# A decoder layer on one core: the first weights on another queue, gamma scaled on another engine, and the FFN input stage in token halves with its activations moved by 64 bytes

## The chip, the core and the metric

The kernel runs on one core of a Trainium2 chip. The metric is the device time of one execution in microseconds (us). The time before is the median of three runs, 662.29 us (661.71 to 663.59).

The core has a tensor engine (PE, its weight loads shown apart as PEld), a vector engine (DVE), a scalar engine (ACT), a general engine (POOL) and a synchronising engine (SP). DMAs are issued by SP, ACT or POOL, each from a queue of its own, in program order.

## The reference

One layer with 512 tokens of 1024 channels, all in float32:

```python
proj = h @ w_in                                  # q | k | v | pool_in | gate logits
mixed = sigmoid(g0) * (moba_attention(q, k, v, rel_bias) @ w_branch_attn) \
      + sigmoid(g1) * (multiscale_pool(p, w_pool_group, pool_scale) @ w_branch_pool)
h = layer_norm(ALPHA * h + mixed @ w_out, ln1_g, ln1_b)
a, u = split(h @ w_ffn_in, 2)                    # 1024 -> 2 x 2816
a = causal_dwconv(a, conv_w, conv_b)             # width 3
f = (gelu(a) * u) @ w_ffn_out                    # 2816 -> 1024
h = layer_norm(ALPHA * h + f, ln2_g, ln2_b)
```

Here `layer_norm` subtracts the mean, multiplies with one over the root of the variance plus epsilon, then with gamma, and adds beta.

## The kernel before

**Matmuls.** Each float32 product is made of three matmuls in float32r, which is a float32 rounded to fewer bits: every operand is split into a rounded part `hi` and a remainder `lo` (`split`, lines 63 to 68: ACT or another engine copies `hi`, DVE subtracts for `lo`), and `mm3` (lines 144 to 148) adds hi x hi, hi x lo and lo x hi in one bank of PSUM. The first argument of a matmul's name in the profile is the moving operand, of 512 or 256 columns, the second the 128x128 stationary one, which every matmul loads anew.

**Weights.** All weights come in chunks of 128 x 1024 in a fixed order (`chunks`, lines 78 to 88). `fetch` (lines 92 to 112) issues a chunk's DMA on SP's queue into one of three raw buffers and splits it into one of five pairs `whi`, `wlo`; `weights` keeps three chunks ahead. The first chunk alone is fetched in two parts of 512 columns, with the second half of the first activations loaded between them.

**Stages, in order.** (1) Start: eight matmuls on zeros warm the array (lines 167 to 169, `WARM`), while the activations `xT` and the first weights land; the v projection (line 240) comes first. (2) The remaining input projections run between the steps of the attention. (3) The branch projections, gated and added into `mx`. (4) The output projection per block of 128 tokens, followed by layer norm 1 (`ln1_vec`) and its transposition into `hT_hi` and `hT_lo` (`ln1_T`), which lie in the pool `hTp` (lines 456 to 459). (5) The FFN input, 44 tiles of 128 output channels: the weights are stationary, `hT` moves. The first five tiles are run over tokens 0 to 255, with the last two transposes between them, then over tokens 256 to 511; tiles 5 to 43 over all 512 tokens at once (lines 609 to 626). After each pair of tiles `gated` makes the convolution, gelu and product. (6) The FFN output as seven products of a Winograd scheme (`PRODUCTS`), whose weights are partly summed by DMA in `tw` (`fetch_fo`, lines 120 to 137; POOL issues those accumulating DMAs). (7) Layer norm 2 per block of 128 tokens: `scale_out`, `share_out` and, for the last block, `finish`.

**Layer norm.** `ln_rows` (lines 447 to 451) loads gamma and beta on POOL's queue to all partitions and multiplies gamma with -0.5 on ACT; it is called ahead of layer norm 1 and in the middle of stage 6, where SP also stores beta to the first 256 rows of the output for `scale_out` to add to. `moments` (lines 470 to 475) aggregates mean and variance on DVE, takes the root of variance plus epsilon on ACT, and adds epsilon to the variance in place on DVE; `invert` refines the inverse root from both.

**What sets the order.** Each engine runs its instructions in an order that the tile framework's scheduler fixes ahead; within `finish` the order is pinned. Semaphores do the rest.

Of the kernel before, what the change touches and what calls it, by code (L numbers as in the profile page):

```python
# [8 lines left out]
F32 = mybir.dt.float32  # L9
F32R = mybir.dt.float32r  # L10
AF = mybir.ActivationFunctionType
ALU = mybir.AluOpType
PSUM = bass.MemoryType.PSUM

P = 128
S = 512
D = 1024
KT = D // P
# [9 lines left out]
EPS = 1e-5  # L28
# [3 lines left out]
LEAD = 3  # L32
RING = 5
TMP = 4
WARM = 8
NKEEP = 12
NLATE = 4
KH = NF // 2
# [5 lines left out]
def layer_kernel(ctx: ExitStack, tc: tile.TileContext, xT, x, w_v, w_c, rel_bias, invcnt, w_group,  # L44
                 pscale, w_br, w_out, lnr, w_fi, convp, w_fo, out):
    nc = tc.nc
# [9 lines left out]
    def bank(name):  # L56
        return ps.tile([P, S], F32, tag="ps", name=name)
# [5 lines left out]
    def split(hi, lo, src, copy=None):  # L63
        if copy:
            copy(hi, src)
        else:
            nc.scalar.activation(hi, src, AF.Copy)  # L67
        nc.vector.tensor_tensor(lo, src, hi.bitcast(F32), op=ALU.subtract)  # L68
# [9 lines left out]
    chunks = [w_v[c] for c in range(4)]  # L78
# [13 lines left out]
    def fetch(pool=None, early=None):  # L92
        i = state["next"]
        state["next"] = i + 1
        if isinstance(chunks[i], tuple):
            ready[i] = fetch_fo(i, *chunks[i])
            return
        raw = wp.tile([P, D], F32, tag="wraw", name=f"wraw{i}", bufs=3)
        if pool is None:
            hi = wp.tile([P, D], F32R, tag="whi", name=f"whi{i}", bufs=RING)  # L100
            lo = wp.tile([P, D], F32R, tag="wlo", name=f"wlo{i}", bufs=RING)
        else:
            hi = pool.tile([P, D], F32R, name=f"whi{i}")
            lo = pool.tile([P, D], F32R, name=f"wlo{i}")
        parts = 2 if early else 1
        for c in range(parts):
            sl = slice(c * (D // parts), (c + 1) * (D // parts))
            nc.sync.dma_start(raw[:, sl], chunks[i][:, sl])
            split(hi[:, sl], lo[:, sl], raw[:, sl])
            if c == 0 and early:  # L110
                early()
        ready[i] = (hi, lo)

    def half(name, sl):
        return w_fo[int(name[1]) - 1, 2 - int(name[2])][:, sl]

    def piece(c):
        return slice(c * D, min((c + 1) * D, KH * S))

    def fetch_fo(i, name, c):  # L120
        sl = piece(c)
        n = sl.stop - sl.start
        step = {"T3": "=B11", "B11": "+B12", "T1": "+B22", "T2": "+B21", "T4": None}
        if name in step:
            raw = tw[:, sl]
        else:
            raw = wp.tile([P, D], F32, tag="wraw", name=f"wraw{i}", bufs=3)[:, :n]
            nc.sync.dma_start(raw, half(name, sl))
        hi = wp.tile([P, D], F32R, tag="whi", name=f"whi{i}", bufs=RING)[:, :n]
        lo = wp.tile([P, D], F32R, tag="wlo", name=f"wlo{i}", bufs=RING)[:, :n]  # L130
        split(hi, lo, raw)
        then = step.get(name)
        if then and then[0] == "+":
            nc.gpsimd.dma_start(raw, half(then[1:], sl), accum_op=ALU.add)  # L134
        elif then:
            nc.sync.dma_start(raw, half(then[1:], sl))
        return hi, lo

    def weights(i):
        while state["next"] <= min(i + LEAD, state["limit"]):  # L140
            fetch()
        return ready[i]

    def mm3(out_, w, a, start, stop, **kw):
        (wh, wl), (ah, al) = w, a
        nc.tensor.matmul(out_, wh, ah, start=start, stop=False, **kw)  # L146
        nc.tensor.matmul(out_, wh, al, start=False, stop=False, **kw)  # L147
        nc.tensor.matmul(out_, wl, ah, start=False, stop=stop, **kw)  # L148

    def split3(v, a):  # L150
        return tuple(t.rearrange("p (a c) -> p a c", a=a) for t in v)

    xT_hi = act.tile([P, KT, S], F32R, tag="actT_hi", name="xT_hi")
    xT_lo = act.tile([P, KT, S], F32R, tag="actT_lo", name="xT_lo")
# [12 lines left out]
    wb_ = bank("warm_ps")  # L167
    for i in range(WARM):
        nc.tensor.matmul(wb_, warm[:, :P], warm, start=True, stop=True)
# [58 lines left out]
    for kt in range(KT):  # L228
        wh, wl = split3(weights(kt // 2), 2)
        wh, wl = wh[:, kt % 2, :], wl[:, kt % 2, :]  # L230
# [189 lines left out]
    for f in range(KT):  # L420
        if f == KT - LEAD:
            state["limit"] = WO0 + RING - 1
        wh, wl = split3(weights(BR0 + f), KT)
# [4 lines left out]
        for br in (1, 0):  # L428
            b = bank(f"br{f}_{br}")
            for k in range(4):  # L430
                src = (zT_hi[:, k, :], zT_lo[:, k, :]) if br else (oT_hi[:, k, :], oT_lo[:, k, :])
                mm3(b, (wh[:, 4 * br + k, :], wl[:, 4 * br + k, :]), src, k == 0, k == 3)
            t = bp.tile([P, S], F32, tag="m", name=f"m{f}_{br}", bufs=4)
# [13 lines left out]
    def ln_rows(r):  # L447
        t = hw.tile([P, 2, D], F32, tag="lnb", name=f"lnb{r}")
        nc.gpsimd.dma_start(t, bass.AP(tensor=lnr.tensor, offset=lnr.offset + r * D, ap=[[0, P], [D, 2], [1, D]]))
        nc.scalar.activation(t[:, 0, :], t[:, 0, :], AF.Copy, scale=-0.5)  # L450
        return t

    lnb = ln_rows(0)
    ypool = ctx.enter_context(tc.tile_pool(name="ypool", bufs=1, reuse_waits="tile"))
    ytiles = [ypool.tile([P, S], F32, name=f"y{j}") for j in range(2)]
    hp = ExitStack()
    hTp = hp.enter_context(tc.tile_pool(name="hTp", bufs=1, reuse_waits="tile"))
    hT_hi = hTp.tile([P, KT, S], F32R, name="hT_hi")
    hT_lo = hTp.tile([P, KT, S], F32R, name="hT_lo")
    st = const.tile([P, NT, 4, 6], F32, name="st")  # L460
# [9 lines left out]
    def moments(i):  # L470
        mu, var = mv[:, i, 0:1], mv[:, i, 1:2]
        nc.vector.bn_aggr(mv[:, i, :], st[:, i].rearrange("p a b -> p (a b)"))
        nc.scalar.activation(rstd[:, i, 0:1], var, AF.Sqrt, bias=eps_t)
        nc.vector.tensor_scalar(var, var, EPS, None, op0=ALU.add)
        return mu, var

    def invert(i, var, pin=lambda ins: ins):
        r, t = rstd[:, i, 0:1], rstd[:, i, 1:2]
# [50 lines left out]
    def ln1_T(i):  # L529
        for n in range(2):  # L530
            b = bank(f"ht{i}_{n}")
            for k in range(4):
                kt = 4 * n + k
                nc.tensor.transpose(b[:, k * P:(k + 1) * P], xs[:, i, kt * P:(kt + 1) * P], ident)
            split(hT_hi[:, 4 * n:4 * n + 4, i * P:(i + 1) * P], hT_lo[:, 4 * n:4 * n + 4, i * P:(i + 1) * P],
                  b.rearrange("p (a c) -> p a c", a=4))
# [29 lines left out]

    def fi_mm(j, b, t):
        wh, wl = split3(weights(FI0 + j), KT)
        for kt in range(KT):
            mm3(b[:, t], (wh[:, kt, :], wl[:, kt, :]), (hT_hi[:, kt, t], hT_lo[:, kt, t]), kt == 0, kt == KT - 1)  # L570

    def gated(j, a, u):
        y = ytiles[j % 2]
        nc.scalar.activation(y, a, AF.Identity, bias=cvp[:, j, 3:4], scale=cvp[:, j, 2:3])
        nc.vector.scalar_tensor_tensor(y[:, 1:], a[:, :S - 1], cvp[:, j, 1:2], y[:, 1:], op0=ALU.mult, op1=ALU.add)
        nc.vector.scalar_tensor_tensor(y[:, 2:], a[:, :S - 2], cvp[:, j, 0:1], y[:, 2:], op0=ALU.mult, op1=ALU.add)  # L576
        nc.scalar.activation(y, y, AF.Gelu)  # L577
        nc.vector.tensor_tensor(fT[:, j, :], y, u, op=ALU.mult)  # L578
# [9 lines left out]
    t1, t2 = slice(0, 256), slice(256, 512)  # L588
# [10 lines left out]
    def formed(j):  # L599
        for c in cuts:  # L600
            if j == c.stop - 1:
                nc.vector.tensor_tensor(rd(c), side(0, c, t1), side(0, c, t2), op=ALU.subtract)
                side_split(0, c, rd(c))
            if j == KH + c.stop - 1:
                nc.vector.tensor_tensor(side(0, c, t2), side(1, c, t2), side(0, c, t2), op=ALU.subtract)
                nc.vector.scalar_tensor_tensor(rd(c), side(1, c, t2), -1.0, rd(c),
                                               op0=ALU.mult, op1=ALU.subtract)

    hb = {}
    for j in range(RING):  # L610
        hb[j] = bank(f"fi{j}")
        fi_mm(j, hb[j], slice(0, 256))
        if j == 0:
            ln1_T(2)
        elif j == RING - 2:
            ln1_T(3)
    for j in range(RING):
        state["limit"] = FI0 + RING + j
        fi_mm(j, hb[j], slice(256, 512))
        if j % 2:  # L620
            gated(j // 2, hb[j - 1], hb[j])
    state["limit"] = len(chunks) - 1
    ra = hw.tile([P, 8, 256], F32, tag="lnb", name="ra")
    for j in range(RING, 2 * NF):
        hb[j] = bank(f"fi{j}")
        fi_mm(j, hb[j], slice(0, S))
        if j % 2:
            f = j // 2
            gated(f, hb[j - 1], hb[j])
            formed(f)  # L630
            if f % 2 == 0 and f >= 6 and f < 6 + 2 * NC:
                c = f // 2 - 3
                nc.sync.dma_start(tw[:, piece(c)], half("B22", piece(c)))
                nc.gpsimd.dma_start(tw[:, piece(c)], half("B12", piece(c)), accum_op=ALU.add)
# [166 lines left out]
```

## Time and profile before

| what | us |
|---|---|
| median of three runs | 662.29 |
| the profiled execution | 663.32 |
| its span, first to last instruction | 661.6 |
| PE busy | 649.4 |
| DVE, ACT, POOL busy | 384.4, 285.9, 89.3 |
| first matmul of the v projection | 5.59 |
| FFN input stage, first to last start | 303.6 to 546.1 |
| last matmul | 652.3 |

The profile is of one execution. A row of the timeline gives start, duration, engine, line, operation, output <- inputs, partitions x elements, and in brackets the idle time ahead of it and what ended that. Rows of the same kind in direct succession are merged (xN). SPq, ACTq are DMA issues. A group row gives the count, then the busy time, the mean duration in ns and the idle time ahead. Durations of matmuls overlap, since they are pipelined; the distance of starts is the rate. All lines are those of the kernel before.

### The profile page before, as it was taken

To read this page: it belongs to the slowest core of one execution; us is meant where nothing else is said; L and a number is where in the kernel's file an instruction comes from. 1 tells how busy PE (TensorE), PEld (TensorE's weight loads), DVE (VectorE), ACT (ScalarE), POOL (GpSimd) and SP (SyncE) were. 2 spreads that over 40 slices of the span, in tenths; PEclk is the share of its full clock that TensorE was granted. 3 is DMA by queue.
4 is the path that set the end of the run, shared out by engine and by line. 5 is a ranking of instruction groups with operands and counts; after the bars stand their busy time and mean duration, and the time that the engine had idled before them with its cause. 6 is when DMAs were issued, how large, how long until landed. Compare 5 with 4: busy or idle time off the path is not lost.

```text
span 661.6 us, 8020 instructions
## 1 busy us (share of the span) xinstructions
PE 649.4 (98%) x3083; PEld 538.8 (81%) x3083; DVE 384.4 (58%) x559; ACT 285.9 (43%) x395; POOL 89.3 (14%) x137
## 2 busy tenths in 40 slices
PE   8999999999999999999999999999999999999994
PEld 6888787877888888889988888888888888888874
DVE  5556665554532675398456344443534548788596
ACT  5646556675422332232443333333323236555452
POOL 0705261211000124002100000000000001124002
PEclk9999999999999999999999999999999999999998
DMA  8643222222322227208942222233233334989905
GB/s 285 215 150 118 80 79 80 73 74 79 96 95 96 93 98 291 91 1 292 251 157 97 96 95 96 95 100 101 99 97 97 104 100 97 211 188 203 261 1 127
DMA packets 24918, 83.70 MB, mean 127 GB/s; under 512 B 3240, under 2 KB 3496, under 8 KB 24624
## 3 DMA queue, kind: packets, MB, share of 16 engines
q1 hardware_dynamic: 19312, 63.77, 29.1%
q0 software_dynamic: 5280, 18.90, 13.2%
q8 instruction: 24, 0.39, 0.2%
q10 hardware_dynamic: 288, 0.52, 0.2%
q14 instruction: 14, 0.11, 0.1%
HBM read 80.01 MB, written 3.17 MB: 126 GB/s over the span
## 4 chain that ended last, share of the span: by engine, by line
PE 77%; issue 10%; DMA 4%; POOL 4%; DVE 3%; ACT 1%; POOLq 0%; DVEq 0%; SPq 0%; ACTq 0%
PE fi L147 11%; PE fi L146 11%; PE fi L148 11%; PE g L146 4%; PE g L147 4%; PE g L148 4%; PE v L240 3%; PE wo L146 2%; PE br L147 2%; PE br L146 2%; PE wo L147 2%; PE wo L148 2%; PE br L148 2%; POOL tw L134 2%; PE ob L372 1%
## 5 line engine op out<-in xcount | busy, mean ns | idle before, releaser
L68 DVE TENSOR_TENSOR wlo<-wraw,whi 128x1024 fp32r<-128x1024 f32 (+1 forms) x105 | 134.3, 1284 | 119.8 <-ACT whi L67 117.9
L67 ACT ACTIVATE whi<-wraw 128x1024 fp32r<-128x1024 f32 (+1 forms) x105 | 109.0, 1041 | 187.4 <-PE fi L147 84.0
L147 PE MATMUL fi<-hT_lo,whi 128*128 128x512 f32 (+1 forms) x392 | 143.8, 367 | 0.0
L148 PE MATMUL fi<-hT_hi,wlo 128*128 128x512 f32 (+1 forms) x392 | 143.8, 367 | 0.0
L146 PE MATMUL fi<-hT_hi,whi 128*128 128x512 f32 (+1 forms) x392 | 143.5, 368 | 0.0
L148 PEld LDWEIGHTS fi<-hT_hi,wlo 128*128 128x128 f32 x392 | 73.9, 189 | 12.3
L147 PEld LDWEIGHTS fi<-hT_lo,whi 128*128 128x128 f32 x392 | 73.9, 189 | 12.0
L146 PEld LDWEIGHTS fi<-hT_hi,whi 128*128 128x128 f32 x392 | 73.6, 189 | 12.2
L134 POOL DMA_DIRECT2D tw<-in_w_fo x18 | 15.8, 906 | 269.9 <-DVE wlo L68 269.9
L146 PE MATMUL g<-xT_hi,whi 128*128 128x512 f32 x128 | 50.3, 393 | 0.0
L148 PE MATMUL g<-xT_hi,wlo 128*128 128x512 f32 x128 | 49.9, 390 | 0.0
L147 PE MATMUL g<-xT_lo,whi 128*128 128x512 f32 x128 | 49.8, 389 | 0.0
L67 ACT ACTIVATE whi<-tw 128x1024 fp32r<-128x1024 f32 (+1 forms) x30 | 29.4, 983 | 25.4 <-PE fi L147 11.3
L578 DVE TENSOR_TENSOR fT<-y,fi 128x512 f32<-128x512 f32 x22 | 15.1, 687 | 40.0 <-PE fi L148 39.2
L68 DVE TENSOR_TENSOR wlo<-tw,whi 128x1024 fp32r<-128x1024 f32 (+1 forms) x30 | 33.3, 1126 | 8.6 <-ACT whi L67 8.4
L577 ACT ACTIVATE y<-y 128x512 f32<-128x512 f32 x22 | 13.9, 632 | 43.0 <-DVE y L576 43.0
L148 PEld LDWEIGHTS g<-xT_hi,wlo 128*128 128x128 f32 x128 | 24.0, 188 | 5.1
L146 PEld LDWEIGHTS g<-xT_hi,whi 128*128 128x128 f32 x128 | 24.0, 188 | 5.0 <-issue 0.2
L147 PEld LDWEIGHTS g<-xT_lo,whi 128*128 128x128 f32 x128 | 24.0, 188 | 4.8
L345 POOL TENSOR_SCALAR pp<-pp,rs 128x128 f32<-128x128 f32 (+3 forms) x32 | 21.8, 698 | 37.7 <-PE g L148 18.4
L146 PE MATMUL wo<-whi,mx_hi 128*128 128x512 f32 x64 | 25.0, 390 | 0.0
L148 PE MATMUL wo<-whi,mx_lo 128*128 128x512 f32 x64 | 24.9, 389 | 0.0
(202 smaller groups left out, 1169.7 us busy)
## 6 DMA issues: line engine op xcount, KB each, us to landing
wraw<-in_w_fi SPq DMA_DIRECT2D x44, 512.0 KB, 3.3
wraw<-in_w_c SPq DMA_DIRECT2D x28, 512.0 KB, 3.4
tw<-in_w_fo POOLq DMA_DIRECT2D x20, 512.0 KB, 7.6
tw<-in_w_fo SPq DMA_DIRECT2D x10, 512.0 KB, 3.9
wraw<-in_w_fo SPq DMA_DIRECT2D x10, 512.0 KB, 5.2
wraw<-in_w_br SPq DMA_DIRECT2D x8, 512.0 KB, 3.3
wraw<-in_w_out SPq DMA_DIRECT2D x8, 512.0 KB, 3.4
strip<-F_d POOLq DMA_DIRECT2D x8, 256.0 KB, 3.5
```

The source lines that it names most:

```text
L67: nc.scalar.activation(hi, src, AF.Copy)
L68: nc.vector.tensor_tensor(lo, src, hi.bitcast(F32), op=ALU.subtract)
L134: nc.gpsimd.dma_start(raw, half(then[1:], sl), accum_op=ALU.add)
L146: nc.tensor.matmul(out_, wh, ah, start=start, stop=False, **kw)
L147: nc.tensor.matmul(out_, wh, al, start=False, stop=False, **kw)
L148: nc.tensor.matmul(out_, wl, ah, start=False, stop=stop, **kw)
L240: nc.tensor.matmul(bs[j], xs_[j][a], (wh, wl)[b], start=kt == 0 and n == 0, stop=False)
L345: nc.gpsimd.tensor_scalar(pp[:, offs[i]:offs[i] + n], pp[:, offs[i]:offs[i] + n], rs[:, i:i + 1], 1.0, op0=ALU.mult, op1=ALU.mult)
L372: nc.tensor.matmul(b[e * DH:(e + 1) * DH, kb * P:], vv[:, kb, h * DH:(h + 1) * DH], PTs[h][:, toff[kb]:toff[kb] + n], start=kb == 0, stop= ...
L577: nc.scalar.activation(y, y, AF.Gelu)
L578: nc.vector.tensor_tensor(fT[:, j, :], y, u, op=ALU.mult)
```

## The change

Five edits: the first chunk's two DMAs are issued by ACT instead of SP, and the copy of its first part is shared, 192 columns on DVE and 320 on ACT; one warm-up matmul fewer; gamma is multiplied with -0.5 by POOL instead of ACT; variance plus epsilon is written to a cell of the statistics `st` instead of in place; the FFN input stage runs each tile over tokens 0 to 255 and then over tokens 256 to 511, and a tile of 64 bytes ahead of `hT_hi` moves `hT_hi` and `hT_lo` by as much.

```diff
-WARM = 8
+WARM = 7
@@ fetch
-            nc.sync.dma_start(raw[:, sl], chunks[i][:, sl])
-            split(hi[:, sl], lo[:, sl], raw[:, sl])
+            (nc.scalar if early else nc.sync).dma_start(raw[:, sl], chunks[i][:, sl])
+            split(hi[:, sl], lo[:, sl], raw[:, sl], fast if early and c == 0 else None)
@@ new, after split3
+    def fast(hi, src):
+        for copy, c in ((nc.vector.tensor_copy, slice(0, 192)), (first_copy, slice(192, 512))):
+            copy(hi[:, c], src[:, c])
+
+    def first_copy(hi, src):
+        nc.scalar.activation(hi, src, AF.Copy)
@@ ln_rows
-        nc.scalar.activation(t[:, 0, :], t[:, 0, :], AF.Copy, scale=-0.5)
+        nc.gpsimd.tensor_scalar(t[:, 0, :], t[:, 0, :], -0.5, None, op0=ALU.mult)
@@ ahead of hT_hi
+    hTp.tile([P, 16], F32, name="hT_gap")
@@ moments
-        nc.vector.tensor_scalar(var, var, EPS, None, op0=ALU.add)
-        return mu, var
+        shifted = st[:, i, 0, 0:1]
+        nc.vector.tensor_scalar(shifted, var, EPS, None, op0=ALU.add)
+        return mu, shifted
@@ fi_mm
-        for kt in range(KT):
-            mm3(b[:, t], (wh[:, kt, :], wl[:, kt, :]), (hT_hi[:, kt, t], hT_lo[:, kt, t]), kt == 0, kt == KT - 1)
+        for c in t:
+            for kt in range(KT):
+                mm3(b[:, c], (wh[:, kt, :], wl[:, kt, :]), (hT_hi[:, kt, c], hT_lo[:, kt, c]), kt == 0, kt == KT - 1)
@@ the calls: first five tiles, the same again, the other 39
-        fi_mm(j, hb[j], slice(0, 256))
+        fi_mm(j, hb[j], (t1,))
-        fi_mm(j, hb[j], slice(256, 512))
+        fi_mm(j, hb[j], (t2,))
-        fi_mm(j, hb[j], slice(0, S))
+        fi_mm(j, hb[j], (t1, t2))
```

`t1` and `t2` are the slices 0 to 256 and 256 to 512.

In the program as built, each engine's order is otherwise the old one, but for these places: on ACT the first DMA stands ahead of the table load and the second behind the dummy activation that follows it; on POOL the second scaling stands between the second and the third of the four accumulating DMAs that follow the load of the rows; on DVE the addition of epsilon moves ahead of the centring.

## The prediction

> **What bounds the kernel now.** I read the page first, then the matmul groups with their shapes kept apart, then the timeline of TensorE for the distance from one start to the next (a matmul's duration overlaps its neighbours and says nothing of the rate), and last the stretches in which TensorE waited.
>
> ```profile
> span 661.6 us, 8020 instructions
> ...
> PE 649.4 (98%) x3083; PEld 538.8 (81%) x3083; DVE 384.4 (58%) x559; ACT 285.9 (43%) x395; POOL 89.3 (14%) x137
> ```
>
> TensorE has work in 98% of the span. Whatever does not change the distance between its matmuls, their number, the start (5.6 us before the first real one), the tail after the last or one of its few waits is worth nothing. The FFN input stage is the largest block; two groups of the lines view give its counts (lines 147 and 148 have the same counts as 146), and rows of the timeline give its rate:
>
> ```profile
> L146 PE MATMUL fi<-hT_hi,whi 128*128 128x512 f32 x312 | 121.4, 389 | 0.0
> L146 PE MATMUL fi<-hT_hi,whi 128*128 128x256 f32 x80 | 22.1, 285 | 0.0
> ```
> ```profile
> 307.46 0.28 PE L147 MATMUL fi<-hT_lo,whi 128*128 128x256 f32 x1
> ...
> 315.85 0.28 PE L148 MATMUL fi<-hT_hi,wlo 128*128 128x256 f32 x1
> ...
> 334.12 0.40 PE L146 MATMUL fi<-hT_hi,whi 128*128 128x512 f32 x1
> ...
> 546.08 0.39 PE L148 MATMUL fi<-hT_hi,wlo 128*128 128x512 f32 x1
> ```
>
> The first two are 70 matmuls apart: 8.39 / 70 = 119.9 ns for 256 columns. The last two are the ends of all 3 x 312 = 936 wide ones, 935 apart: 211.96 / 935 = 226.7 ns for 512. There is no idle time in either. The slope is (226.7 - 119.9) / 256 = 0.417 ns a column, so 512 columns are 213.6 ns and 256 are 106.8, and **13.1 ns stand on top of every matmul**, whatever its width. That is 31 to 32 columns' worth.
>
> **The halves, the large term.** 936 wide matmuls become 1872 of 256 columns; the 240 that are halves already stay. At the rates above the pair costs 239.8 instead of 226.7, so 936 x 13.1 = 12.3 us more. That is the price if the 13.1 ns stay as they are. The 64 bytes decide whether they do. What the trace says of the 13.1 ns:
>
> ```profile
> 7.47 1.05 PE L240 MATMUL v<-whi,xT_hi 128*128 128x512 f32 x2
> 8.32 1.02 PE L240 MATMUL v<-wlo,xT_hi 128*128 128x512 f32 x2
> 9.18 0.62 PE L240 MATMUL v<-whi,xT_lo 128*128 128x512 f32 x2
> 9.63 0.63 PE L240 MATMUL v<-wlo,xT_hi 128*128 128x512 f32 x2
> ```
> ```profile
> 67.12 1.09 PE tr L359 x10
> ```
>
> Before 9.18 the array still runs at its slow start pace: two matmuls in 0.85 us, 425 ns each, which is twice 213 with nothing on top. Those matmuls also load new weights each time, so the 13.1 ns are no fixed price of changing weights; they lie in the supply of the moving operand and hide when the array takes two times as long over a column. And 31 to 32 columns of 4 bytes are 125 to 128 bytes of a partition. In the built program hT_hi lies at byte 101056 of a partition, 64 past a multiple of 128, as do the moving operands of all other matmuls here except the transposes; a row of 512 or 256 columns then touches 17 or 9 blocks of 128 bytes where 16 or 8 would do. The gap tile puts hT_hi at 101120 and hT_lo at 117504, both multiples of 128. My reading is that the extra block is the 13.1 ns, and that it goes. No row of this trace shows an aligned moving operand of 256 columns, so both ends stay: 119.9 ns if nothing goes, 106.8 if all goes. The nearest row with an aligned one is the transposes (moving operand ident, at a multiple of 128; 128 columns of new weights each): ten in 1.09 us, 109 ns, with only 128 columns to stream, so I read it as the floor that loading 128 columns of weights sets. I take 109. The 2112 half matmuls then cost 2112 x 0.109 = 230.2 us against 936 x 0.2267 + 240 x 0.1199 = 241.0 now: **-10.8 us**. VectorE, ScalarE and the weight transfers have room for a tile every 5.2 us instead of 5.4 (they are 58% and 43% busy).
>
> The Trainium skill, "TensorE: Matmul & The Clock Gate", section "Back-to-back issue gap", gives N/2.4 + 2.5 ns: 215.8 for 512 and 109.2 for 256 columns, hence an estimate of 936 x 2.5 = 2.3 us more for the halves. The rows disagree with both of its figures as the operands lie now, and the rows are what I count from. The same skill, "SBUF — State Buffer", section "Specifications (TRN2)", gives lines of 16 bytes; by that a move of 64 bytes changes nothing, which speaks against the gap and for the first rival below. No row here shows a moved operand.
>
> **The start.**
>
> ```profile
> 0.82 0.38 SPq L172 DMA_DIRECT2D xr<-in_xT  x1
> 1.25 0.42 SPq L108 DMA_DIRECT2D wraw<-in_w_v  x1
> 2.10 0.20 ACT L164 ACTIVATE dummy<-eps_t 128x1 f32<-128x1 f32 x1
> 4.91 0.63 ACT L67 ACTIVATE whi<-wraw 128x512 fp32r<-128x512 f32 x1 [2.60 <-DMA wraw<-in_w_v]
> 5.59 1.22 PE L240 MATMUL v<-whi,xT_hi 128*128 128x512 f32 x2 [0.73 <-ACT whi L67]
> 9.97 1.06 ACT L67 ACTIVATE whi<-wraw 128x1024 fp32r<-128x1024 f32 x1 [1.35 <-DMA wraw<-in_w_v]
> ```
>
> The first half of the weights is issued as ScalarE's first instruction, ahead of its table load, so about when SP issues now (0.82 instead of 1.25, 0.43 us). The copy goes from 0.63 us for 512 columns to 320 (by the 0.63 and 1.06 rows 0.84 ns a column: 0.16 less), with VectorE's 192 beside it. TensorE starts 0.59 us earlier if the data comes that much earlier. The second half's DMA stands behind the table load and the dummy, at 2.3 instead of 2.2; its columns are wanted 12 matmuls later, after 9.6, so that is hidden. Everything behind is fed earlier, since SP loses two issues. Bounds: 0.4 lost (one warm-up matmul fewer, and the fast pace that begins at 9.18 comes later), 1.3 won (seven warm-ups end near 4.3). I take **-0.6**.
>
> **Gamma on POOL.**
>
> ```profile
> 604.65 0.56 POOL L449 DMA_DIRECT2D lnb<-in_lnr  x1 [1.31 <-DVE sd_lo L68]
> 610.38 1.76 POOL L134 DMA_DIRECT2D tw<-in_w_fo  x2 [1.73 <-DVE wlo L68]
> 613.88 1.73 SPq L711 DMA_DIRECT2D out<-lnb  x2
> 613.95 1.06 ACT L450 ACTIVATE lnb<-lnb 128x1024 f32<-128x1024 f32 x1 [4.25 <-DMA lnb<-in_lnr]
> 614.91 1.04 ACT L67 ACTIVATE sd_hi<-fT 128x1024 fp32r<-128x1024 f32 x1
> 618.37 3.74 SPq L128 DMA_DIRECT2D wraw<-in_w_fo  x3
> ```
> ```profile
> 626.66 1.06 ACT L67 ACTIVATE whi<-wraw 128x1024 fp32r<-128x1024 f32 x1 [6.91 <-DMA wraw<-in_w_fo]
> 632.43 0.39 PE L146 MATMUL foe<-whi,sd_hi 128*128 128x512 f32 x1
> 633.48 0.50 PE L147 MATMUL fod<-wlo,sd_hi 128*128 128x512 f32 x1 [0.66 <-DVE wlo L68]
> ```
>
> ScalarE stands 4.25 us for the second pair of rows, and behind it the splits that free the raw weight buffers. SP's next three weight transfers go out at 618.37 only, land about 8 us later, and the last splits come late: TensorE starts at 633.48 instead of 632.66. Counting 0.1 for the slower first matmul, 0.9 us. With the scaling on POOL ScalarE goes on at 610; SP still waits for the rows until 613.88 for its two stores, then issues the weights at about 615.6, 2.8 us earlier, and the wait goes: **-0.9**. On POOL the new instruction waits for the same landing, and two transfers of tw stand behind it, which slip from 610.4 to about 616 (1024 columns at twice the 816 ns of the row below). They are read from 637.44 on, so 20 us cover them. The first pair of rows is scaled at 265.01 now and used at 283.44, which covers POOL's 1.6 us.
>
> ```profile
> L345 POOL TENSOR_SCALAR pp<-pp,rs 128x512 f32<-128x512 f32 x8 | 6.5, 816 | 0.0
> 265.01 1.04 ACT L450 ACTIVATE lnb<-lnb 128x1024 f32<-128x1024 f32 x1
> 283.44 1.40 DVE L485 SCALAR_TENSOR_TENSOR xs<-xs,mv,lnb 128x512 f32<-128x512 f32 x2
> 637.44 1.06 ACT L67 ACTIVATE whi<-tw 128x1024 fp32r<-128x1024 f32 x1 [0.30 <-PE fod L148]
> ```
>
> **The variance in its own cell.**
>
> ```profile
> 653.58 0.26 DVE L472 BATCH_NORM_AGGREGATE mv<-st 128x2 f32<-128x24 f32 x1
> 653.87 0.30 ACT L473 ACTIVATE rstd<-mv,eps_t 128x1 f32<-128x1 f32 x1 [1.77 <-DVE mv L472]
> 654.20 0.15 DVE L474 TENSOR_SCALAR mv<-mv 128x1 f32<-128x1 f32 x1 [0.36 <-ACT rstd L473]
> 654.27 0.74 DVE L485 SCALAR_TENSOR_TENSOR xs<-xs,mv,lnb 128x512 f32<-128x512 f32 x1
> ```
>
> In the tail VectorE adds epsilon in place, so it waits until ScalarE has read the variance: 0.36 us. The sum now goes to st, which nothing reads any more, and the chain behind it moves up: **-0.3**. Elsewhere this wait lies under TensorE's work.
>
> **Sum.** The profiled execution took 663.3 us, its span 661.6. 663.3 - 10.8 - 0.6 - 0.9 - 0.3 = 650.7. That execution is 1.0 above the median of the three runs (662.3), so the forecast for a median is **649.7 us**. With 107 to 111 ns for the half matmul (4.2 either way) and the bounds of the start it lies between 645 and 655.
>
> **Rivals.**
> 1. *The 13.1 ns belong to every matmul, wherever its operand lies.* For it: they are the same at both widths in every stage, and no row shows them gone at full pace with wide matmuls. Against it: the slow-pace rows and the 128 bytes. Then only the doubling is left: 663.3 + 12.3 - 1.8 = 673.8, or 672.8 for a median, slower. It decides from the distance at which the stage and the small gains cancel: 2112 p = 241.0 + 1.8, p = 115 ns.
> 2. *Only the 64 bytes in excess go, half a block*: 6.6 ns of 13.1 remain, 113.4 ns a half, 226.8 a pair. The wide part stays as it is, the 240 halves gain 1.6: 663.3 - 1.6 - 1.8 = 659.9, 658.9 for a median.
> 3. *The small edits do not do what they say*: the two queues share the same transfer engines, the first weights land no earlier, and SP's stores still hold up the late weights. The 1.5 us are then missing: 651.2. This lies within the forecast's own range.
>
> **Chances.** The forecast with rival 3 has 0.50, rival 1 0.37, rival 2 0.09, and 0.04 is left for others. About 0.3% is what a measurement of this kernel can tell from no change. Faster by more than that: 0.50 + 0.09 less a little for values between, 0.57; within: 0.04; slower: 0.39. The range has to take in both signs: from 646 to 674, which leaves out less than 2 in 10; the likeliest case's own range is 645 to 655.
>
> **What would show it.** In the changed trace, the distance between two half matmuls of the FFN input: 109 for me, 120 for rival 1, 113 for rival 2; its 2112 matmuls over 230 or 253 us. The first matmul on weights near 5.0 instead of 5.59, no wait of TensorE in the last but one product, and no idle time of VectorE before the sum with epsilon in the tail. I am wrong if weight loads, not the moving operand, set the 119.9 ns, or if alignment plays no part.

## The result, and the profile after

| | median us | range, runs |
|---|---|---|
| before | 662.26 | 661.71 to 663.59, 6 runs |
| changed | 668.12 | 667.41 to 670.18, 6 runs |

The changed kernel is **slower by 5.9 us**: ratio 1.0087, 95% interval 1.0072 to 1.0102. The forecast was 649.7. The profiled execution took 667.4 us.

The page of the changed kernel, its span and its engines (lines of the changed kernel stand up to nine further down in the code; `mm3` stays at 146 to 148):

```profile
span 665.6 us, 9888 instructions
...
PE 654.7 (98%) x4018; PEld 581.8 (87%) x4018; DVE 385.0 (58%) x560; ACT 284.3 (43%) x393; POOL 94.6 (14%) x139
```

TensorE is still the bound, with 5.3 us more of work and 935 more matmuls on record. The groups of the FFN input stage, shapes kept apart: only half matmuls are left, 3 x 704, and the durations of their weight loads, which overlap, add up to 396 us where three groups of 392 added up to 221. The two lines are one of the three groups each, of the matmuls and of the loads.

```profile
L147 PE MATMUL fi<-hT_lo,whi 128*128 128x256 f32 x704 | 196.9, 280 | 0.0
...
L147 PEld LDWEIGHTS fi<-hT_lo,whi 128*128 128x128 f32 x704 | 132.2, 188 | 0.0
```

The rate, from TensorE's timeline (start, duration, line, operation). These two rows are 2014 matmuls apart, with no idle time between them:

```profile
314.33 0.28 PE L147 MATMUL fi<-hT_lo,whi 128*128 128x256 f32 x1
...
551.53 0.28 PE L148 MATMUL fi<-hT_hi,wlo 128*128 128x256 f32 x1
```

237.20 / 2014 = **117.8 ns** for 256 columns. The forecast said 109, its first rival 120, the point at which the sign turns 115. From its first start to its last start and one distance more the stage lasts 250.5 us (301.14 to 551.65) instead of 242.7 (303.60 to 546.31): +7.8 us.

The last but one product, and the tail:

```profile
619.86 0.86 SPq L721 DMA_DIRECT2D out<-lnb  x2
619.93 3.09 POOL L457 TENSOR_SCALAR lnb<-lnb 128x1024 f32<-128x1024 f32 x1 [5.90 <-DMA lnb<-in_lnr]
620.82 5.36 SPq L128 DMA_DIRECT2D wraw<-in_w_fo  x3
...
637.81 0.39 PE L146 MATMUL foe<-whi,sd_hi 128*128 128x512 f32 x1
638.04 0.39 PE L147 MATMUL fod<-wlo,sd_hi 128*128 128x512 f32 x1
```
```profile
657.99 0.26 DVE L480 BATCH_NORM_AGGREGATE mv<-st 128x2 f32<-128x24 f32 x1
658.29 0.29 ACT L481 ACTIVATE rstd<-mv,eps_t 128x1 f32<-128x1 f32 x1 [1.77 <-DVE mv L480]
658.29 0.15 DVE L483 TENSOR_SCALAR st<-mv 128x1 f32<-128x1 f32 x1
658.36 0.74 DVE L494 SCALAR_TENSOR_TENSOR xs<-xs,mv,lnb 128x512 f32<-128x512 f32 x1
```

Between foe and fod TensorE now goes on after 0.23 us where 1.05 passed; in the tail the sum with epsilon starts with the square root and not 0.33 us behind it. Both small terms did what was said; the stage of the halves cost more than they gave.

### The profile page after: what moved, and what is told of

The parts are those of the page before. It is cut to its first block, busy times and chain, and to the rows that moved or that the text cites. A ratio compares the mean times of both kernels' runs of the same rounds, so it can differ in the third digit from the quotient of the medians.

```text
span 665.6 us, 9888 instructions
## 1 busy us (share of the span) xinstructions
PE 654.7 (98%) x4018; PEld 581.8 (87%) x4018; DVE 385.0 (58%) x560; ACT 284.3 (43%) x393; POOL 94.6 (14%) x139
## 3 DMA queue, kind: packets, MB, share of 16 engines
q10 hardware_dynamic: 576, 1.05, 0.4%
## 4 chain that ended last, share of the span: by engine, by line
PE 94%; DVE 2%; POOL 2%; ACT 1%; DMA 0%; issue 0%; DVEq 0%; ACTq 0%; POOLq 0%
PE fi L147 13%; PE fi L146 12%; PE fi L148 12%; PE g L146 4%; PE g L148 4%; PE g L147 4%; PE v L247 3%; PE wo L147 2%; PE br L148 2%; PE br L147 2%; PE wo L148 2%; PE wo L146 2%; PE br L146 2%; PE foa L148 2%; PE foa L146 2%; PE fod L148 2%
## 5 line engine op out<-in xcount | busy, mean ns | idle before, releaser
L147 PE MATMUL fi<-hT_lo,whi 128*128 128x256 f32 x704 | 196.9, 280 | 0.0
L148 PE MATMUL fi<-hT_hi,wlo 128*128 128x256 f32 x704 | 196.3, 279 | 0.0
L146 PE MATMUL fi<-hT_hi,whi 128*128 128x256 f32 x704 | 196.0, 279 | 0.0
L147 PEld LDWEIGHTS fi<-hT_lo,whi 128*128 128x128 f32 x704 | 132.2, 188 | 0.0
L146 PEld LDWEIGHTS fi<-hT_hi,whi 128*128 128x128 f32 x704 | 132.0, 188 | 0.0
L148 PEld LDWEIGHTS fi<-hT_hi,wlo 128*128 128x128 f32 x704 | 131.7, 187 | 0.0
```

## The experiments

Theories: the prediction's own step, which the expectations call the record's (a block of 128 bytes too many, 13.1 ns a matmul, gone with the gap); **rival 1** (13.1 ns belong to every matmul); and, from the trace after, **A** (the place of the moving rows costs about 2 ns at any width) and **B** (at 256 columns the weight loads set the distance, and places matter only as the two reads stand against each other). Where a distance is worked out, the two rows quoted for it come from TensorE's timeline.

### The gap alone

```diff
+    hTp.tile([P, 16], F32, name="hT_gap")
```

> The kernel before with hT laid 64 bytes further on, and nothing else; tiles 5 to 43 of the FFN's input stage keep 512 tokens. Theory A (the place of the moving operand costs about 2 ns a matmul at any width): the 512-column matmuls of tiles 5 to 43 go from 226.7 to about 224.6 ns, the 256-column ones of tiles 0 to 4 from 119.9 to about 117.8, so 936 x 2.1 + 240 x 2.1 = 2.5 us less, about 659.8 us. Theory B (the weight loads set the distance at 256 columns and only they feel the place): 512 columns stay at 226.7, 256 columns go to 117.8, 0.5 us less, about 661.8. The record's own step (a whole block of 13.1 ns) would have given 213.6 ns at 512 columns and 12 us less.

Measured: 663.3 us against 662.3, ratio 1.0014 (1.0001 to 1.0027).

```profile
314.53 0.28 PE L147 MATMUL fi<-hT_lo,whi 128*128 128x256 f32 x1
...
331.25 0.28 PE L148 MATMUL fi<-hT_hi,wlo 128*128 128x256 f32 x1
331.37 0.40 PE L146 MATMUL fi<-hT_hi,whi 128*128 128x512 f32 x1
...
545.39 0.39 PE L148 MATMUL fi<-hT_hi,wlo 128*128 128x512 f32 x1
```

142 distances at 256 columns: 16.72 / 142 = 117.7 ns. 935 at 512: 214.02 / 935 = **228.9 ns, 2.2 more than before**. All three expectations are missed at 512 columns; at 256 the 117.8 of A and B holds. A multiple of 128 makes the wide matmul slower and the half one faster by 2.2 ns, so an extra block of 128 bytes is not what the 13.1 ns are.

### The halves alone

```diff
-        for kt in range(KT):
+        for c in t:
+            for kt in range(KT):
...
-        fi_mm(j, hb[j], slice(0, S))
+        fi_mm(j, hb[j], (t1, t2))
```

> The kernel before with tiles 5 to 43 of the FFN's input stage in two halves of 256 tokens, hT where it was. Theory A (halves cost by their fixed part, the gap takes 2.1 ns of it): 119.9 ns a half matmul, 1872 x 119.9 - 936 x 226.7 = +12.3 us, about 674.5 us. Rival (the 117.8 ns of the changed kernel come from the order in halves, not from the place): 117.8 ns, +8.3 us, about 670.6.

Measured: 674.0 us, ratio 1.0172 (1.0158 to 1.0186), 11.7 us more than before.

```profile
315.11 0.28 PE L147 MATMUL fi<-hT_lo,whi 128*128 128x256 f32 x1
...
556.79 0.28 PE L148 MATMUL fi<-hT_hi,wlo 128*128 128x256 f32 x1
```

241.68 / 2014 = 120.0 ns. Halving costs what rival 1 said; the order in halves does not lower it. The gap is what takes 120.0 to 117.8 in the changed kernel: 2112 x 2.2 = 4.6 us.

### Where the rows lie, five ways

The same 64 bytes ahead of the weight tiles, which moves all that lies behind on that side:

```diff
+    wp.tile([P, 16], F32, name="w_gap")
```

> The kernel before with 64 bytes put ahead of the weight tiles, which moves the weights and all tiles that lie behind them on that side by 64 bytes, hT among them. The moving operand then lies at 0 modulo 128 in the v and FFN input stages and the stationary one at 0 or 64 by stage; in the FFN input stage both lie at 0. Theory A (place of the moving operand alone): FFN input 224.6 ns at 512 columns and 117.8 at 256, v likewise 224.6 at the full clock, while the q and k stages (moving still at 64, stationary at 0) stay at 226.7; about 3 to 4 us less in all. Theory B (only where the two lie against each other counts): FFN input as before, 226.7 and 119.9, since both moved together. Theory C (the stationary operand's place counts too): q and k change as well.

Measured: 665.4 us, ratio 1.0046 (1.0029 to 1.0063).

```profile
318.81 0.28 PE L148 MATMUL fi<-hT_lo,whi 128*128 128x256 f32 x1
...
335.84 0.28 PE L149 MATMUL fi<-hT_hi,wlo 128*128 128x256 f32 x1
335.96 0.40 PE L147 MATMUL fi<-hT_hi,whi 128*128 128x512 f32 x1
...
547.92 0.39 PE L149 MATMUL fi<-hT_hi,wlo 128*128 128x512 f32 x1
```

Both operands moved together: 17.03 / 142 = 119.9 and 211.96 / 935 = 226.7 ns, as before to the digit, though the moving rows now lie at a multiple of 128. Theory A falls. The loss comes from other stages: the q, k, pool and gate projections, moving rows at 64 and stationary ones at 0, take 233 ns. The first 24 matmuls of q, 23 distances in 5.36 us:

```profile
27.26 0.39 PE L147 MATMUL q<-xT_hi,whi 128*128 128x512 f32 x1
...
32.62 0.40 PE L149 MATMUL q<-xT_hi,wlo 128*128 128x512 f32 x1
```

And in the last product (moving 0, stationary 64) 256-column matmuls come every 113.3 ns, 39 distances in 4.42 us:

```profile
649.05 0.28 PE L147 MATMUL fo_cut<-whi,sd_hi 128*128 128x256 f32 x1
...
653.47 0.28 PE L147 MATMUL fo_cut<-whi,sd_hi 128*128 128x256 f32 x1
```

That is half of 226.7, and each of these matmuls still loads 128 columns. At 512 columns the stages that came to lie the same way in this run (v, the output projection, the products fob and foe) take 228.8 to 229.0 ns, as the FFN input does with the gap alone. Three more places of hT: a gap of 32 bytes, one of 96, and the two tiles of 64 bytes together.

```diff
+    hTp.tile([P, 8], F32, name="hT_gap")
```
```diff
+    hTp.tile([P, 24], F32, name="hT_gap")
```
```diff
+    wp.tile([P, 16], F32, name="w_gap")
...
+    hTp.tile([P, 16], F32, name="hT_gap")
```

> The kernel before with hT laid 32 bytes further on instead of 64; the FFN's input tiles 5 to 43 stay 512 wide. The record's step (reads in blocks of 128 bytes): moving rows at 96 modulo 128 still touch one block more, so 226.7 and 119.9 ns as before. Theory B (what counts is where the moving rows lie against the stationary ones, by which the two reads disturb each other): a third pair of numbers, neither 226.7 and 119.9 (both at the same place) nor 228.9 and 118.0 (64 bytes apart); its direction isn't known, anything from 213 to 235 ns at 512 columns.

> The same with hT laid 96 bytes further on, moving rows at 32 modulo 128. The record's step: 226.7 and 119.9 ns, one block too many as before. Theory B: again a pair of its own, between that of 32 bytes and that of 64 bytes if the disturbance changes steadily, anywhere from 213 to 235 ns if not.

> The kernel before with the 64 bytes ahead of the weights and 64 more ahead of hT: in the FFN's input stage the moving rows lie at 64 and the stationary ones at 0 modulo 128, as in the q and k stages of the run with 64 bytes ahead of the weights. Theory B: 233.3 ns at 512 columns as there, 936 x 6.6 = 6 us more than that run's stage. Theory A (place of the moving rows alone): 226.7 and 119.9 as before, since the moving rows are where they were.

Measured, one execution each: 667.0, 666.7 and 668.1 us, against 661.7 before. The rows of the 32-byte gap, as an example (142 and 935 distances again):

```profile
314.31 0.28 PE L147 MATMUL fi<-hT_lo,whi 128*128 128x256 f32 x1
...
330.88 0.28 PE L148 MATMUL fi<-hT_hi,wlo 128*128 128x256 f32 x1
331.00 0.39 PE L146 MATMUL fi<-hT_hi,whi 128*128 128x512 f32 x1
...
549.16 0.39 PE L148 MATMUL fi<-hT_hi,wlo 128*128 128x512 f32 x1
```

| moving, stationary rows, bytes modulo 128 | 512 columns, ns | 256 columns, ns |
|---|---|---|
| 64, 64 (before) | 226.7 | 119.9 |
| 0, 0 (weights and hT moved) | 226.7 | 119.9 |
| 0, 64 (gap of 64) | 228.9 | 117.7 |
| 64, 0 (both tiles) | 228.9 | 117.8 |
| 96, 64 (gap of 32) | 233.3 | 116.7 |
| 32, 64 (gap of 96) | 233.3 | 120.0 |

In this stage only the place of the two against each other counts, as theory B has it. Nothing goes below 226.7 at 512 columns, a mean over 935 distances, where the kernel before stood. But B's figure for the last of these runs was missed (233.3 expected from the q stage, 228.9 measured), so the difference modulo 128 isn't all that matters.

Whether 256 bytes more change that, on the changed kernel:

```diff
-    hTp.tile([P, 16], F32, name="hT_gap")
+    hTp.tile([P, 80], F32, name="hT_gap")
```

> The changed kernel with the gap at 320 bytes instead of 64: the moving rows stay at 0 modulo 128 but move by 256 bytes against the stationary ones modulo 512. If only the place modulo 128 counts: 117.8 ns a half matmul and about 668.1 us, as changed. If the place modulo 512 counts (the last product's 256-column matmuls took 113.3 ns with moving and stationary rows 192 bytes apart modulo 512, the FFN's 118.0 with 448 apart): 113.3 ns, 2016 x 4.5 = 9 us less, about 659.1 us.

Measured: 667.7 us, ratio to before 1.0092 (1.0075 to 1.0109), and 117.8 ns as in the changed kernel. The place modulo 512 is not what gives the last product its 113.3.

### Half the weights to load

```diff
+            m = slice(0, 64 if kt % 4 else P)
-            mm3(b[:, t], (wh[:, kt, :], wl[:, kt, :]), ...
+            mm3(b[m, t], (wh[:, kt, m], wl[:, kt, m]), ...
```

> The kernel before with fewer stationary columns in the FFN's input stage: in 6 of 8 slices of the contraction only 64 of the 128 columns are loaded and multiplied (half of the output rows then lack those terms; the moving rows stay as they are). Theory S (the moving stream alone sets 226.7 ns at 512 columns, and a weight load under way takes it from 113.3 to 119.9 at 256): 226.7 and about 113 ns. Theory F (13.1 ns belong to every matmul, however it is laid): 226.7 and 119.9. Theory L (each weight load takes its time out of the moving stream): half the load gives back half of it, about 220 and 113.3 ns.

Measured: 663.4 us in one execution, against 662.1 before. First the group of the shortened weight loads, then TensorE's rows:

```profile
L146 PEld LDWEIGHTS fi<-hT_hi,whi 128*64 128x64 f32 x294 | 39.5, 134 | 18.3
```
```profile
315.12 0.28 PE L146 MATMUL fi<-hT_hi,whi 128*64 128x256 f32 x1
...
315.80 0.28 PE L146 MATMUL fi<-hT_hi,whi 128*128 128x256 f32 x1
...
331.05 0.40 PE L146 MATMUL fi<-hT_hi,whi 128*128 128x512 f32 x1
...
545.58 0.39 PE L148 MATMUL fi<-hT_hi,wlo 128*64 128x512 f32 x1
```

With a load of 134 instead of about 190 ns, the 256-column matmul falls from 119.9 to 0.68 / 6 = **113.3 ns**, the moving rows being where they were. These six are the second and third shortened slice behind a full one; in the first it takes 116.7. The 512-column one does not fall: 214.53 / 935 = 229.4 with three loads in four halved, against 226.7, and single distances lie between 224 and 236 by slice. The edit also multiplies 64 columns instead of 128, so the load is not the only thing that it changes.

So the 13.1 ns were two things. At 256 columns 6.6 of them go with the shorter load; they are no fixed price of a full load, since the last product above comes every 113.3 ns with loads of 128 columns, its operands lying otherwise. The rest goes by the column: 226.7 / 512 = 113.3 / 256 = 0.443 ns. Theory S holds at 256 columns for two of the three shortened slices; at 512 it holds in that less loading gives nothing back, while the extra 2.7 ns were not expected.

### The small edits, together and apart

All but the halves and the gap (in the changed kernel):

```diff
-    hTp.tile([P, 16], F32, name="hT_gap")
-        fi_mm(j, hb[j], (t1, t2))
+        fi_mm(j, hb[j], (slice(0, S),))
```

> The changed kernel without the two large edits: hT where it was before, tiles 5 to 43 over all 512 tokens; the start, gamma on POOL and the cell of the variance stay changed. If the three terms of the record hold (0.6 at the start, 0.9 at the last-but-one product, 0.3 in the tail), 1.8 us less than before, about 660.4 us; if the end only follows TensorE's matmuls and the start's gain is lost to the clock, about 1.0 less, 661.3.

Measured: **660.0 us, ratio 0.9963 (0.9949 to 0.9976)**, faster than both kernels. Then, from the kernel before, the start alone and gamma alone, each with its lines of the change's diff (`WARM`, `fetch`, `fast`, `first_copy` for the one, `ln_rows` for the other):

> The kernel before with the start of the change alone: the first weights over ACT's queue, their copy split over VectorE and ScalarE, 7 warm-up matmuls. The record's term: 0.6 us less, 661.7 against 662.3; first matmul of the v stage near 5.0 us. If the TensorE clock decides and is granted no earlier: no change.

> The kernel before with the scaling of gamma on POOL and nothing else. The record's term: TensorE's 1.0 us wait in the last but one product goes, 0.9 us less, 661.4 against 662.3. If another split takes the place of the late one: the wait stays near 1 us and the time is the same.

The start alone: 662.4 against 662.1, ratio 1.0000 (0.9988 to 1.0012). Gamma alone: 660.9, ratio 0.9978 (0.9966 to 0.9991). The timeline of gamma alone shows its path:

```profile
614.20 1.32 SPq L711 DMA_DIRECT2D out<-lnb  x2
614.27 3.23 POOL L450 TENSOR_SCALAR lnb<-lnb 128x1024 f32<-128x1024 f32 x1 [5.76 <-DMA lnb<-in_lnr]
615.61 5.05 SPq L128 DMA_DIRECT2D wraw<-in_w_fo  x3
...
632.29 0.39 PE L146 MATMUL foe<-whi,sd_hi 128*128 128x512 f32 x1
632.52 0.39 PE L147 MATMUL fod<-wlo,sd_hi 128*128 128x512 f32 x1
```

SP issues the weights at 615.61 instead of 618.37, and TensorE's wait of 1.05 us is gone.

In the start, ScalarE's copy of the first weights and the first matmul on them, first with the start alone, then with the start untouched (the next run):

```profile
3.99 0.47 ACT L158 ACTIVATE whi<-wraw 128x320 fp32r<-128x320 f32 x1 [1.24 <-DMA wraw<-in_w_v]
4.28 0.25 DVE L155 CAST whi<-wraw 128x192 fp32r<-128x192 f32 x1
...
4.68 0.76 PE L247 MATMUL v<-whi,xT_hi 128*128 128x512 f32 x1 [0.24 <-DVE whi L155]
```
```profile
3.91 0.63 ACT L67 ACTIVATE whi<-wraw 128x512 fp32r<-128x512 f32 x1 [1.61 <-DMA wraw<-in_w_v]
...
4.59 0.80 PE L240 MATMUL v<-whi,xT_hi 128*128 128x512 f32 x1
```

The weights land no earlier over ACT's queue, and TensorE now waits for VectorE's share. In eight profiles of kernels with the old start the first matmul came at 4.50 to 4.67, in two (that of before and that of gamma alone) at 5.59 and 5.43; with the new start, in four, at 4.68 to 4.91. In the two late ones the fast pace of the array began at 9.0 and 9.2 us, in the other twelve, old start or new, between 4.9 and 7.3. The one profile from which the forecast read the start was one of the late ones.

Last, gamma and the variance's cell (`ln_rows` and `moments`), without the new start:

> The kernel before with gamma scaled on POOL and the separate cell of the variance, its start, its halves and its gap left alone. Gamma alone gave 1.3 us, the cell should add 0.3 to 0.4 in the tail: about 660.6 us against 662.3. If the start of the change is worth its 0.6 us on top, this stays 0.6 above the run with all three small edits (660.0); if the start is worth nothing, the two agree within what can be measured (1 us).

Measured: 660.3 us, ratio 0.9973 (0.9962 to 0.9983). From the first of the last 45 half matmuls to the end of the span it takes 14.1 us, in this profile and in the three others with the cell, and 14.5 before (14.4 to 14.7 with the start or gamma alone): the cell is worth about 0.4. The new start adds nothing that can be told from no change.

## Why the prediction was wrong

**The halves, the failed step.** The forecast counted -10.8 us from a half matmul at 109 ns; it took 117.8, and the stage cost 7.8 us more. The step that failed is "My reading is that the extra block is the 13.1 ns, and that it goes". It went wrong in two places.

*The split into slope and fixed part.* (226.7 - 119.9) / 256 = 0.417 ns a column takes for granted that one limit holds at both widths. It doesn't: shorter loads bring a half matmul down to 113.3 and a wide one not at all, so at 256 columns the load adds to the distance as the operands lie here, and at 512 it doesn't show. The trace before had a sign of it. Of the two stretches below, the first has half matmuls and the second wide ones; the columns are the window, its length, then the busy time of PE and of the weight loads (PEld), which have no idle time in the first and 17% in the second:

```profile
core 0: us, PE busy (x) PEld busy (x) DVE busy (x) ACT busy (x) POOL busy (x), PEclk, DMA share, GB/s
307.26:315.97 8.71, 8.71 (x76) 8.71 (x74) 5.13 (x13) 1.23 (x3) 3.58 (x4) 1.00 1.05 363
...
334.28:524.25 189.97, 189.97 (x839) 157.33 (x839) 92.12 (x100) 63.41 (x74) 0.00 (x0) 1.00 0.31 100
```

A full load path alone doesn't fix the distance, since the last product with the moved weights has one too (4.42 of 4.42 us) at 113.3. With 0.443 ns a column nothing is left on top of a wide matmul, and two halves at the lowest distance that any run shows only equal it (2 x 113.3 = 226.6).

*The 128 bytes.* That 13.1 ns are worth about 128 bytes at the column rate was a coincidence. Moving both operands by 64 bytes changed nothing (226.7, 119.9); moving hT alone made wide matmuls slower by 2.2 ns. The record named what would make it wrong, "if weight loads, not the moving operand, set the 119.9 ns, or if alignment plays no part"; the first holds in part (6.6 ns, at this placing), and of the second this much, that a multiple of 128 has no virtue of its own.

What holds of its argument from the slow start pace: a wide matmul takes 427 ns there, less than twice 226.7, so not all of the 226.7 scales with the pace. That nothing is on top there leans on 213.6, which comes from the same split, and isn't shown. A supply of moving columns that doesn't speed up with the array would give both figures; this is argued, not shown. The 109 ns that the prediction took from the transposes as the floor of a 128-column load was not reached by any half matmul: the lowest mean is 113.3.

The prediction's figures from the Trainium skill, "TensorE: Matmul & The Clock Gate", section "Back-to-back issue gap" (215.8 and 109.2 ns), stand there for an isolated matmul; of a stream of weight loads and matmuls the same section of the Trainium skill says that both set the spacing. The runs agree with this at 256 columns (119.9 with full loads, 113.3 with short ones), and no run reaches either figure: the lowest mean distances of these float32r matmuls are 226.7 and 113.3. By the Trainium skill, "SBUF — State Buffer", section "Specifications (TRN2)", its 16-byte lines would leave a move of 64 bytes without effect; the runs show +2.2 and -2.2 ns.

**Rival 1** had the mechanism half right: its +12.3 us for the halves alone was +11.7 in the medians. Its "wherever its operand lies" was not: the gap gave 4.6 us of it back, and the stage is 7.8 longer. **Rival 2** foresaw 113.4 ns, a value that the loads could give but the gap didn't.

**The start**, -0.6, is not there (ratio 1.0000). The step took a late landing in one profile for the rule, and the earlier issue for an earlier landing. That part of rival 3, "the first weights land no earlier", was right.

**Gamma**, -0.9: right in mechanism, down to the issue of the weights ("at about 615.6", measured 615.61); 1.3 us in the medians, 0.6 to 2.3 by the interval, and 0.95 in the profile of gamma alone (the stretch from the first fod matmul of that product to the first of the next product, 620.96 to 636.15 against 621.11 to 637.25).

**The cell**, -0.3: right, about 0.4.

Sum with the measured terms: 662.3 + 7.8 - 1.3 - 0.4 = 668.4; measured 668.1.

Open: why the place of one operand against the other moves the distance by up to 6.6 ns, for 32 and 64 bytes in opposite directions at the two widths; why the projections from xT take 233 ns where hT at the same places modulo 128 takes 228.9; and why the last product reaches 113.3 where the FFN input stays at 117.7. For the second there is a candidate: in the built programs the moving rows lie 64 bytes past the stationary ones modulo 256 wherever 228.9 was measured, and 192 past them in those projections. No run changed that by itself.

## What to carry to other kernels

A fixed cost read off two widths is only as good as the assumption that one engine path limits both; look whether the narrower one is already short of time for its weight loads before dividing the difference. An offset that "explains" a number by its size should be tested by moving both operands, not only the one suspected. And a term at the start of a kernel needs several profiles: one landing late by 0.9 us made an edit look worth 0.6 that was worth nothing.

## What was not expected of the hardware

- These float32r matmuls stream at 0.443 ns a column after the start (512 in 226.7, 256 in 113.3), while at the slow start pace 512 take 427 ns (1.71 us for four, from 7.47 to 9.18), 0.83 a column. The granted clock in the trace reads 1.00 in both.
- A 64-byte move of one operand against the other changes the distances of a whole stage: 226.7 to 228.9 ns at 512 columns, to 233.3 for 32 or 96 bytes, and to between 116.7 and 120.0 at 256 (119.9 before). Four projections that no edit was meant for lost 3 per cent (226.7 to 233) when 64 bytes were put ahead of the weights.
- With the operands as they lay before, loading 64 instead of 128 weight columns took 6.6 ns off most of the 256-column matmuls concerned (119.9 to 113.3); with the operands 64 bytes apart in the last product, full loads left 113.3 too.
